# A hybrid decoder layer on one core: the first attention groups moved in the input projection, and the loads at the start of the last stage placed anew

## The chip, the core and the metric

The kernel runs on one core of a Trainium2 chip. The core has TensorE (PE in the profile; its weight loads are PEld), VectorE (DVE), ScalarE (ACT), GpSimd (POOL) and SyncE (SP), which work side by side and wait for each other through semaphores. DMA transfers are issued by SP, ACT or POOL; each of these works through its instructions in order, so a transfer that has to wait holds up all that its engine was given after it. The metric is the time of one execution on the device in microseconds (us); smaller is better.

## The reference

One layer of a decoder for 4096 new tokens of width 1024 and 64 sampled ones, in float32:

```python
h = _rmsnorm(x, g_pre)
z = h @ w_in                                   # 1024 x 2816
cb, cc, ch, cg, q, k, v, ag, mq, mg = _split_cols(z)
u = cc * ch                                    # A: gated short convolution, 256 channels
out_a = silu(cg) * cb * conv3(u)
o_b = window_attention(q, k, v, sink)          # B: 8 query heads, 2 key heads of 64, window 128
out_b = silu(ag) * o_b
o_c = memory_attention(mq, mk, mv)             # C: 4 heads of 64 into 256 memory tokens
out_c = silu(mg) * o_c
y = concat([out_a, out_b, out_c]) @ w_out      # 1024 x 1024
x = x + _rmsnorm(y, g_post)
```

Besides the new rows it returns the last keys, values and convolution rows, and the memory's keys and values.

## The kernel before

Every float32 product is made of three matmuls on a high and a low part of its operands: ACT casts the high part (`hi`, `mh`, `wo` first half), DVE subtracts for the low part (`lo`, `ml`, `wo` second half).

**The input projection** goes over 8 blocks of 520 tokens in three phases; each block and phase takes seven products of a fast matrix scheme (`PRODUCTS`). In the third phase a product has three quads of 12 matmuls (`product`, L381), so a step, one product of one block, has 36. Steps are numbered `n = 7 * (b - 1) + p` from -7 to 48 (`third_jobs`). Work of other kinds is hung into a step: a job of slot 0, 1 or 2 is written behind quad 0, 1 or 2. `evict` (L388) adds the accumulators into z on DVE; `finish_parts` casts z into two parts and stores them to `qd`, `finish_v` to `vd`, `finish_gate` and `finish_conv` to `md`. `v_load` and `v_turn` turn the value rows in steps `V_TURNS` and store them to `vn`.

**Attention** works on 16 chunks of 256 tokens, two groups of 128 queries each. A chunk's keys and queries are loaded by `chunk_load` (one issue for `kst`, two or four for `q`, all on POOL), its gates by `load_mix` (`mix`, or `place` for even chunks). Chunk 0 and the odd chunks share one buffer for keys and one for queries (`third["pre"]`). A group passes through these pieces:

- `bands` and `crosses`: scores on TensorE (`ws`, `xs`); `band_out` copies the window scores into the group's tile `s`, a copy on ACT (L1242) and a masked one on DVE (L1246);
- `band_max`, `band_exps`, `band_weights`, `cross_max`, `cross_exps`, `cross_weights`: softmax; the last is on POOL (L1295);
- `turn_band` (L1303) and `turn_cross` (L1307): DVE transposes 32 x 32 squares within `s`, and 16 transfers of 64 KB carry the squares into the tile `w` (L1312);
- `masks` (L1322): four selects on POOL that mask `w` and make `wd`;
- `values` (L1095, `pv`): products with the values (`vh` for loaded value rows, `halves`), then the gates are multiplied in.

`s` lives in one of two tiles: `pair` (single buffer of the pool `work`) for groups 0, 1, 2 and all even ones, the pool `sp` for the odd ones from 3. A new `s` waits until the 16 transfers of the last one have left. The transfers go through POOL for groups 0 and 1 and through SP from group 2 on.

Groups 0, 1 and 2 do all but the last pieces within the third phase: `EARLY` gives the step at which a group opens, `STAGES` and `PIECES` the steps after it.

**The last stage** takes 33 blocks of 128 rows (`Block.run`). A block is 48 matmuls of 128 x 512 (L1616, `y`), in two halves p of eight k with three products each. `events_of(i, block)` writes other work ahead of product k of half p. `values_and_scores(i)` makes the scores of group i + 3 and the values of group i + 1 (at the start of a block from block 2 on; after k = 2 in block 0, k = 3 in block 1). `turn(0, g)`, `turn(1, g)` and `turn(2, g)` are the two transposes and the masks. `split` makes `mh` and `ml` of a block's mixed rows; those of block 1 have their low part on POOL, all others on DVE. `query_loads` brings the later chunks from within `scores`. The output weights are loaded on POOL by `wo_load` in the last eight steps (raw tiles `wor`, the last three in the buffers `hx` of the input tiles) and split by `wo_split`, whose low part is on POOL for four of 16 tiles. `open_attention` lays the pools of the last stage over those of the projection; the first pool lies over `hx`.

The instructions of DVE, PE, SP, ACT and POOL stand in the order in which they are written (`written_order`), in the third phase and after it.

## Time and profile before

| | |
|---|---|
| median of three runs | 1494.8 us (1493.6 to 1497.38) |
| profiled execution | 1495.91 us, span 1494.2 us |
| granted clock of TensorE, mean | 0.997 |
| instructions | 30887 |
| third phase ends, last stage begins | at 945.6 us of the span |

The profile records one execution; its times count from the first instruction. A row of the timeline has start, length, engine, line, operation, output <- inputs, shape and how often; in brackets stands how long the engine had been idle and what ended that. SPq is SP's issuing of transfers. A row of stretches has the stretch, its length, the busy time of PE, PEld, DVE, ACT and POOL with the number of instructions, the granted clock, the DMA share and GB/s. A row by line has the least, median and greatest length in ns. Matmuls overlap and their ends are modelled, so PE shows as busy in places where it runs slowly.

### The profile page before, as it was taken

What the parts mean: (1) busy time and instruction counts of PE and PEld (TensorE: products, weight loads), DVE (VectorE), ACT (ScalarE), POOL (GpSimd) and SP (SyncE); (2) the same over time, 40 slices, a digit from 0 to 9 for tenths busy, and PEclk for the clock granted to TensorE, in tenths of its full rate; (3) what the DMA queues carried; (4) which work ended last, traced back from release to release, by engine and by line L of the source; (5) the groups of instructions that cost most, each with busy time, mean ns of one, the idle gap of its engine ahead of it and who ended that gap; (6) DMA issues with size and microseconds to landing.
All of it is one profiled execution on the core that took longest, in us unless ns stands there. A gap on an engine that the chain in (4) does not pass through costs nothing.

```text
span 1494.2 us, 30887 instructions
## 1 busy us (share of the span) xinstructions
PE 1465.3 (98%) x11459; PEld 1338.3 (90%) x11459; DVE 1209.0 (81%) x1888; ACT 758.4 (51%) x1869; POOL 447.4 (30%) x611
## 2 busy tenths in 40 slices
PE   9999999999999999999999999889999999999998
PEld 9999999999999999999999989767777777777766
DVE  6779888898987877797677768978988888888853
ACT  6776566466422222244545435645655655655542
POOL 0222332212300000000000332555556555565541
PEclk9999999999999999999999999999999999999999
DMA  9989999886864333257898987999999998899673
GB/s 256 195 241 226 292 288 275 229 286 241 236 204 145 135 122 129 100 216 229 281 287 273 291 259 242 326 234 224 215 250 221 235 234 222 211 222 243 203 205 109
DMA packets 213788, 337.27 MB, mean 226 GB/s; under 512 B 55301, under 2 KB 127365, under 8 KB 213605
## 3 DMA queue, kind: packets, MB, share of 16 engines
q1 hardware_dynamic: 159621, 226.42, 51.7%
q0 software_dynamic: 44944, 77.10, 21.0%
q10 hardware_dynamic: 9072, 31.77, 6.9%
q8 instruction: 91, 1.49, 0.5%
q14 instruction: 60, 0.49, 0.1%
HBM read 192.48 MB, written 110.15 MB: 203 GB/s over the span
## 4 chain that ended last, share of the span: by engine, by line
PE 63%; DMA 18%; DVE 7%; SPq 4%; issue 4%; POOL 2%; ACT 2%; ACTq 0%; POOLq 0%; DVEq 0%
PE c L381 46%; PE y L1616 11%; DMA w<-s 6%; SPq L1312 3%; PE pv L1095 3%; DMA mix<-md 2%; DMA xr<-in_x_p 1%; DMA place<-md 1%; PE ws L1095 1%; PE mem_acc L809 1%; DMA o_yp<-xr 1%; DMA vh<-vn 1%; DVE z L388 1%; DMA svm<-in_cmv 1%; DMA vd<-v 1%
## 5 line engine op out<-in xcount | busy, mean ns | idle before, releaser
L1616 PE MATMUL y<-wo,mh 128*128 128x512 f32 (+1 forms) x1040 | 329.3, 391 | 1.0 <-DVE s L1246 0.5
L388 DVE TENSOR_TENSOR z<-c,z 128x520 f32<-128x520 f32 (+1 forms) x308 | 193.6, 642 | 78.1 <-PE c L381 74.3
L1616 PEld LDWEIGHTS y<-wo,mh 128*128 128x128 f32 x1040 | 194.2, 188 | 54.3 <-DVE wmx L1255 5.0
L1616 PE MATMUL y<-wo,ml 128*128 128x512 f32 (+1 forms) x520 | 201.2, 387 | 0.5 <-POOL ml L1591 0.5
L1295 POOL TENSOR_SCALAR s<-s,xrd 128x256 f32<-128x256 f32 x128 | 61.2, 493 | 214.3 <-DVE xrd L1292 154.5
L1616 PEld LDWEIGHTS y<-wo,ml 128*128 128x128 f32 x520 | 97.8, 188 | 19.4 <-POOL ml L1591 0.9
L1265 ACT ACTIVATE s<-s,wnm 128x128 f32<-128x128 f32 x256 | 98.7, 387 | 0.0
L1242 ACT COPY s<-ws 128x256 f32<-128x256 f32 x128 | 41.1, 378 | 98.6 <-PE ws L1095 64.4
L1646 POOL TENSOR_TENSOR xr<-yn,xr 128x1024 f32<-128x1024 f32 x31 | 74.5, 2403 | 27.7 <-ACT yn L1645 22.7
L754 POOL MEMSET negs<- 128x1 f32 x1 | 0.1, 99 | 269.1 <-PE c L381 269.1
L1624 ACT ACTIVATE y<-y 128x512 f32<-128x512 f32 (+1 forms) x66 | 38.6, 585 | 58.4 <-DVE yn L1623 57.5
L1322 POOL TENSOR_SCALAR_AFFINE_SELECT wd<-w 128x512 f32<-128x512 f32 x64 | 52.9, 827 | 50.2 <-DMA w<-s 30.9
L1246 DVE COPY_PREDICATED s<-wmask,ws 128x256 f32<-128x256 uint8 x124 | 47.9, 439 | 21.4 <-ACT s L1242 20.0
L1623 DVE TENSOR_TENSOR yn<-y,gpost 128x512 f32<-128x512 f32 (+1 forms) x66 | 44.8, 679 | 21.8 <-PE y L1616 20.2
L1095 PEld LDWEIGHTS ws<-kst,q 64*128 64x128 f32 x768 | 48.2, 186 | 14.6 <-issue 9.9
L1095 PE MATMUL ws<-kst,q 64*128 64x256 f32 x768 | 56.0, 289 | 3.0 <-DVE s L1246 2.6
L1288 ACT ACTIVATE s<-xs,xnm 128x256 f32<-128x256 f32 x128 | 58.1, 461 | 1.0 <-DVE xnm L1282 1.0
L1322 POOL TENSOR_SCALAR_AFFINE_SELECT w<-w 128x512 f32<-128x512 f32 x64 | 56.1, 895 | 2.2
L390 ACT COPY z<-c 128x520 f32<-128x520 f32 (+1 forms) x44 | 24.4, 554 | 56.1 <-PE c L381 53.6
L1645 ACT ACTIVATE yn<-yn,yst 128x1024 f32<-128x1024 f32 x31 | 35.7, 1150 | 33.2 <-POOL yst L1637 33.2
L1265 ACT ACTIVATION_READ_ACCUMULATOR s<-s,wnm 128x1 f32 x256 | 47.9, 187 | 0.0
L185 POOL DMA_DIRECT2D md<-th x48 | 26.2, 548 | 64.8 <-DVE th L442 40.6
(957 smaller groups left out, 4986.9 us busy)
## 6 DMA issues: line engine op xcount, KB each, us to landing
w<-s SPq DMA_DIRECT2D x480, 64.0 KB
q<-qd POOLq DMA_DIRECT2D x30, 768.0 KB, 8.8
xr<-in_x_p SPq DMA_DIRECT2D x32, 512.0 KB
nat<-in_x_p SPq DMA_DIRECT2D x39, 416.0 KB
o_yp<-xr SPq DMA_DIRECT2D x31, 512.0 KB
md<-th POOLq DMA_DIRECT2D x48, 260.0 KB, 6.2
qd<-zh SPq DMA_DIRECT2D x48, 260.0 KB
qd<-z SPq DMA_DIRECT2D x48, 260.0 KB
```

The costliest lines, as they stand in the source:

```text
L381: TE.matmul(bank[:, :HW], l, r, start=first and i == 0, stop=last and i == 3 * KH - 1)
L388: add = lambda dst, other: V.tensor_tensor(dst, c, other, op=ALU.add)
L1095: ins = TE.matmul(o, w, x, **kw)
L1246: V.copy_predicated(to, squares(third["wmask"]), squares(s3[:, :, 0:P]))
L1265: S.activation(sm[:, h], sm[:, h], AF.Exp, bias=nm[:, h : h + 1], scale=SCALE, accum_out=den[:, h : h + 1])
L1288: S.activation(p[:, i], s[:, i].rearrange("p (a k j) -> p a k j", a=2, k=4), AF.Exp, bias=nm[:, i : i + 1], scale=SCALE, accum_out=den[:, ...
L1295: G.tensor_scalar(p[:, i], p[:, i], rd[:, i : i + 1], 0.5, op0=ALU.mult, op1=ALU.mult)
L1312: (DMA if b > 1 else G).dma_start(to[32 * k : 32 * k + 32, g], self.squares[32 * g : 32 * g + 32, k])
L1322: G.affine_select(out, src, pattern=[[32 * sign, 2], [0, 8], [sign, 32]], compare_op=op, fill=0.0, base=base * sign, channel_multiplier=-s ...
L1616: TE.matmul(acc, self.hl[l][:, k], wo[k][c0 // 512][:, r, c0 % 512 : c0 % 512 + c1 - c0], start=j == 0, stop=j == passes * KT - 1)
L1623: V.tensor_tensor(yn[:m, c0:c1], acc[:m], gpost[0][:m, c0:c1], op=ALU.mult)
L1646: total = G.tensor_tensor(self.xr, yn, self.xr, op=ALU.add)
```

## The change

- **First groups.** `EARLY` opens groups 0, 1 and 2 at steps 14, 23 and 33 in place of 17, 27 and 37. The transposes come in the stages 5 and 6 after it in place of 6 and 7, masks at 9 in place of 10, values at 14 and 15 in place of 16; the eight exponentials are split 6 and 2 in place of 4 and 4.
- **Their loads.** Chunk 0's keys and queries are loaded at step 10 (were in `first_chunk`, step 14), its values and gates at 12, `early_values` at step 20 (was 16), chunk 1 at 26 (was 29).
- **Buffers and queues.** Group 2's 16 transfers go through POOL in place of SP. From group 3 on the two tiles for `s` are exchanged: odd groups take `pair`, even ones `sp`; the sample's scores (`ssm`) move from `pair` to `sp`. In `open_attention` the pools `mixp` and `sp` change places, so that `mixp` is now the first.
- **End of the projection.** In the last step the weight tiles 14 and 15 are split in slot 2 in place of slot 1. The value rows 2 and 3 (`half_load`) are loaded before the last pending stores, and the pool `vp` is opened there.
- **Start of the last stage.** Chunk 2 is loaded before mix 1, and mix 1 through POOL in place of SP. Chunk 3 is loaded in block 0 (was block 1), mix 2 ahead of k = 6 of block 1's first half (was its second half). The low part of block 1 is computed on DVE.

```diff
-                            (14, 0, first_chunk), (16, 0, lambda: chunks[0].early_values()), (29, 0, lambda: chunk_load(1))):
+                            (10, 2, lambda: chunk_load(0)), (12, 0, first_chunk), (20, 2, lambda: chunks[0].early_values()), (26, 0, lambda: chunk_load(1))):
...
-    EARLY = {0: 17, 1: 27, 2: 37}
+    EARLY = {0: 14, 1: 23, 2: 33}
...
-              (3, 0, of("band_exps", range(0, 4))), (3, 0, of("early_cross_max")), (4, 0, of("band_exps", range(4, 8))),
-              (5, 0, of("early_cross_exps")), (5, 0, of("band_weights")), (6, 0, of("early_cross_weights")), (6, 0, of("turn_band")),
-              (7, 0, of("turn_cross")))
-    PIECES = {0: (*STAGES, (10, 0, of("masks")), (16, 0, of("values"))), 1: (*STAGES, (10, 0, of("masks")), (16, 0, of("values"))),
-              2: (*STAGES, (10, 0, of("masks")))}
+              (3, 0, of("band_exps", range(0, 6))), (3, 0, of("early_cross_max")), (4, 0, of("band_exps", range(6, 8))),
+              (4, 0, of("early_cross_exps")), (4, 1, of("band_weights")), (5, 0, of("early_cross_weights")), (5, 0, of("turn_band")),
+              (6, 0, of("turn_cross")), (9, 0, of("masks")))
+    PIECES = {0: (*STAGES, (14, 0, of("values"))), 1: (*STAGES, (15, 0, of("values"))), 2: STAGES}
...
-        chunk_load(0)
         chunk = chunks[0]
...
-                    slots[(0, 0, 1, 1)[n] if p == 6 else (0, 1, 1, 2)[n]].append(lambda j=j: wo_split(j))
+                    slots[(0, 0, 2, 2)[n] if p == 6 else (0, 1, 1, 2)[n]].append(lambda j=j: wo_split(j))
...
+        nonlocal vp
+        vp = ctx.enter_context(tc.tile_pool(name="vp", bufs=4, side="right"))
+        for n in range(2, 4):
+            half_load(n)
         for i in sorted(pending):
...
-        sp, bp, wd0 = left("sp"), left("bp"), left("wd0")
+        mixp, bp, wd0 = left("mixp"), left("bp"), left("wd0")
         left("gap").tile([P, NS], F32, name="gap")
-        bq, yq, wl, wd1, mixp, yp = left("bq"), left("yq"), left("wl"), left("wd1"), left("mixp"), left("yp", 2)
+        bq, yq, sp, wl, wd1, yp = left("bq"), left("yq"), left("sp"), left("wl"), left("wd1"), left("yp", 2)
...
-            (G if self.c == 2 else DMA).dma_start(self.mix, md[:, :, self.ts].rearrange("k p n -> p k n"))
+            (G if 0 < self.c < 3 else DMA).dma_start(self.mix, md[:, :, self.ts].rearrange("k p n -> p k n"))
...
-            t = sp.tile([P, 2 * D], F32, tag="s", name=f"s{b}") if b % 2 and b > 1 else pair(f"s{b}")
+            t = pair(f"s{b}") if b % 2 or b < 3 else sp.tile([P, 2 * D], F32, tag="s", name=f"s{b}")
...
-                    (DMA if b > 1 else G).dma_start(to[32 * k : 32 * k + 32, g], self.squares[32 * g : 32 * g + 32, k])
+                    (DMA if b > 2 else G).dma_start(to[32 * k : 32 * k + 32, g], self.squares[32 * g : 32 * g + 32, k])
...
-        ssm = pair("ssm")
+        ssm = sp.tile([P, 2 * D], F32, tag="s", name="ssm")
...
-                (G if b == 1 else V).tensor_tensor(lo, src, f(hi), op=ALU.subtract)
+                V.tensor_tensor(lo, src, f(hi), op=ALU.subtract)
...
+    chunk_load(2)
     chunks[1].load_mix()
-    chunk_load(2)
-    for n in range(2, 4):
-        half_load(n)
...
+        if i == 0:
+            at(1, 1, chunk_load, 3)
         if i == 1:
-            at(1, 1, chunk_load, 3)
-            at(1, 1, lambda: chunks[2].load_mix())
+            at(0, 6, lambda: chunks[2].load_mix())
```

More of the change, by code (lines that the diff above doesn't have):

```diff
@@ L1055, in open_attention @@
     def open_attention():
-        nonlocal ps, mixp, wp, wl, vp, bp, bq, yp, yq, sp
+        nonlocal ps, mixp, wp, wl, bp, bq, yp, yq, sp
         own.close()
@@ L1062, in open_attention @@
         ps = {tag: ctx.enter_context(tc.tile_pool(name=f"ps{tag}", bufs=1, space=bass.MemoryType.PSUM)) for tag in (*range(4), "pv", 4, 5)}
-        vp = ctx.enter_context(tc.tile_pool(name="vp", bufs=4, side="right"))
         left = lambda name, bufs=1: att.enter_context(tc.tile_pool(name=name, bufs=bufs))
-        sp, bp, wd0 = left("sp"), left("bp"), left("wd0")
+        mixp, bp, wd0 = left("mixp"), left("bp"), left("wd0")
         left("gap").tile([P, NS], F32, name="gap")
-        bq, yq, wl, wd1, mixp, yp = left("bq"), left("yq"), left("wl"), left("wd1"), left("mixp"), left("yp", 2)
+        bq, yq, sp, wl, wd1, yp = left("bq"), left("yq"), left("sp"), left("wl"), left("wd1"), left("yp", 2)
         wp = wd0, wd1
```

## The prediction, made before the changed kernel ran

> **What bounds the kernel now.** I read the page's busy row first, then TensorE's own rows in order of time, kept to those with idle time before them (and four without, used below), then the stretches around the places found.
>
> ```profile
> PE 1465.3 (98%) x11459; PEld 1338.3 (90%) x11459; DVE 1209.0 (81%) x1888; ACT 758.4 (51%) x1869; POOL 447.4 (30%) x611
> ```
> TensorE is the bound, and the change touches no matmul. It can move the time only through TensorE's idle time and the slow clock after it. Nearly all of what it can reach sits in two places.
>
> ```profile
> 892.80 1.50 PE L1095 MATMUL ws<-kst,q 64*128 64x256 f32 x12 [2.56 <-DVE s L1246]
> ...
> 945.60 0.39 PE L1616 MATMUL y<-wo,mh 128*128 128x512 f32 x1
> ...
> 951.06 0.98 PE L1095 MATMUL xs<-mk,q 64*128 64x256 f32 x11 [1.45 <-DVE z L388]
> 956.21 0.50 PE L1616 MATMUL y<-wo,mh 128*128 128x512 f32 x1 [0.52 <-DVE s L1246]
> 962.65 0.50 PE L1616 MATMUL y<-wo,ml 128*128 128x512 f32 x1 [0.48 <-POOL ml L1591]
> 965.39 0.38 PE L1095 MATMUL ws<-kst,q 64*128 64x256 f32 x2
> 966.12 1.58 PE L1095 MATMUL ws<-kst,q 64*128 64x256 f32 x22 [0.35 <-DMA q<-qd]
> 968.10 0.97 PE L1095 MATMUL xs<-mk,q 64*128 64x256 f32 x11 [0.28 <-DVE s L1246]
> 971.73 0.65 PE L1095 MATMUL pv<-w,vh 128*64 128x256 f32 x4 [1.21 <-DMA vh<-vn]
> 981.30 0.98 PE L1095 MATMUL ws<-kst,q 64*128 64x256 f32 x12
> 984.43 1.09 PE L1095 MATMUL pv<-w,mv 128*64 128x128 f32 x16 [0.72 <-ACT y L1624]
> 1005.80 1.44 PE L1095 MATMUL pv<-w,mv 128*64 128x128 f32 x16 [4.63 <-ACT y L1624]
> ...
> 1021.06 1.69 PE L1095 MATMUL ws<-kst,q 64*128 64x256 f32 x24
> ```
> ```profile
> 887.00:900.00 13.00, 10.44 (x77) 9.86 (x76) 7.24 (x14) 4.37 (x8) 2.85 (x4) 0.87 0.78 249
> 1000.00:1011.00 11.00, 6.37 (x57) 4.05 (x56) 5.55 (x12) 4.72 (x17) 5.11 (x6) 0.84 1.48 314
> 972.50:982.50 10.00, 10.00 (x64) 7.91 (x62) 8.70 (x16) 6.10 (x25) 5.16 (x5) 1.00 0.40 99
> 987.00:1012.00 25.00, 20.31 (x133) 15.12 (x126) 14.75 (x33) 13.48 (x52) 15.41 (x18) 0.93 1.37 299
> ```
>
> The bracket is the idle time and what ended it; in the stretches the third number from the end is the granted clock, the last two are DMA share and GB/s. Steps of the third phase are counted back from 945.6, 36 matmuls each. The first wait is in step 38: 2.56 us idle and 13.00 x (1 - 0.87) = 1.7 us of slow clock, 4.25 us. The other eight, blocks 0 to 3 of the last stage, are 9.64 us, with 11.00 x (1 - 0.84) = 1.8 us of slow clock after the longest. Together 15.7 us, 1.0% of the time.
>
> **The change part by part.** *First groups.* The wait in step 38: group 2's scores go into the one buffer that group 1 used, and group 1's 16 transfers had not left it.
>
> ```profile
> 872.73 1.24 DVE L1307 STREAM_TRANSPOSE s<-s 128x1024 f32<-128x1024 f32 x1
> ```
> ```profile
> 874.57 7.15 POOL L1312 DMA_DIRECT2D w<-s  x14 [3.96 <-DVE z L424]
> ```
> ```profile
> 891.90 0.37 ACT L1242 COPY s<-ws 128x256 f32<-128x256 f32 x1 [7.39 <-DMA w<-s]
> ```
>
> From the transpose's end (873.97) to the copy (891.90) are 17.9 us. That made TensorE 2.56 us late, so 15.4 us would have been in time, over three steps. The change puts group 1's turn at step 29 and group 2 at step 33: four steps, some 4.3 us more. The wait is gone: -4.25 us. But group 0 turns at step 20 and group 1 opens at 23: three steps again. What did group 0 take before (turn at 24)?
>
> ```profile
> 824.05 1.24 DVE L1307 STREAM_TRANSPOSE s<-s 128x1024 f32<-128x1024 f32 x1
> ```
> ```profile
> 839.21 1.54 POOL L1322 TENSOR_SCALAR_AFFINE_SELECT wd<-w 128x512 f32<-128x512 f32 x2 [2.31 <-DMA w<-s]
> ```
>
> 825.29 to 839.2: 13.9 us, in time. Step 20, though, is the last product of its block, as step 34 was and step 24 was not; the stores that follow it and the value-row loads one and three steps later (the turns at 23 and 25, at 37 and 39) fall beside the transfers in both. So I take step 34's 17.9 us as the nearer row: 17.9 - 15.4 - 0.4 (the two value transposes that now lie inside) = 2.1 us of wait at step 24. Whether the slow clock follows lies between the 1.45 us wait, after which none shows, and the 2.56 us wait, after which it does; I take half of 1.7. Term +3.0 us, between 0 (by 13.9) and +5.3 (by the 19.4 us of group 4 below, with the clock). The six steps in place of eight and the split of the exponentials move the same instructions; TensorE had no wait on them and DVE has room (a stretch of steps 20 to 23 is 14.04 us busy of 17.4). I put this at nothing.
>
> ```profile
> 803.50:820.90 17.40, 17.40 (x147) 17.40 (x146) 14.04 (x25) 12.88 (x36) 0.98 (x3) 1.00 0.79 260
> ```
>
> *Chunk 0, its values and chunk 1 sooner.* These loads had landed without a wait of TensorE, and come sooner now; nothing.
>
> *Group 2's turn at 39, its masks at 42, its transfers from SP to POOL.* Before, they fell into steps 44 to 48 and POOL stood behind them:
>
> ```profile
> 947.18 1.84 POOL L1322 TENSOR_SCALAR_AFFINE_SELECT wd<-w 128x512 f32<-128x512 f32 x2 [6.11 <-DMA w<-s]
> 949.09 2.17 POOL L1322 TENSOR_SCALAR_AFFINE_SELECT w<-w 128x512 f32<-128x512 f32 x2
> 951.23 3.41 POOL L204 TENSOR_TENSOR wo<-wor,wo 128x512 fp32r<-128x512 f32 x2
> 954.94 0.74 POOL L1128 DMA_DIRECT2D kst<-qd  x1 [0.30 <-POOL wo L204]
> ```
> ```profile
> 954.67 1.20 ACT L1242 COPY s<-ws 128x256 f32<-128x256 f32 x4 [3.00 <-POOL wo L204]
> ```
> ```profile
> 947.47 2.08 DVE L204 TENSOR_TENSOR wo<-wor,wo 128x512 fp32r<-128x512 f32 x2
> ...
> 950.59 0.42 DVE L388 TENSOR_TENSOR z<-c,z 128x260 f32<-128x260 f32 x1
> ```
>
> POOL waited 6.11 us for the transfers, so its share of the output weights and chunk 2's loads came late, and group 3's scores, laid over those weights' raw tiles, waited 3.00 us on ACT. With masks at 42 and group 3 in the other buffer this chain is gone: the 0.52 us and 0.35 us waits with it. The two weight splits of 2.08 us now stand behind the last eviction (950.59), which then ends about 2 us sooner, more than the 1.45 us it was late. The low part of block 1 goes to DVE, where the others take 1.2 us:
>
> ```profile
> L1591 DVE TENSOR_TENSOR ml<-place,mh x15: 1181/1184/1648, 944.5 to 1426.3; 128x1024 fp32r<-128x1024 f32 x15
> L1591 POOL TENSOR_TENSOR ml<-place,mh x1: 2404/2404/2404, 960.2 to 960.2; 128x1024 fp32r<-128x1024 f32 x1
> ```
>
> DVE, full until 957, is relieved by more than it is given: 0.48 us gone. Value rows 2 and 3 are asked for before the last stores, two issues on SP of some 0.6 us that the stores wait for and nobody behind them: 1.21 us gone. Term: 1.45 + 0.52 + 0.48 + 0.35 + 1.21 = -4.0 us; were DVE still late, -2.0. On POOL group 2's 16 issues (0.51 each) stand ahead of its masks alone, which wait for them anyway. Chunk 2's five, mix 1 (from SP) and chunk 3's three, 0.74 to 0.85 us each, are some 7 us ahead of group 3's weights and the next block's output; POOL has given up 2.40 us of low part and does the 4.01 us of masks and most of the 3.41 us of weights earlier, so I count nothing, and 1 us within the bounds above if that cover is thin.
>
> *Chunk 3 and mix 2.* They stood behind group 3's masks on POOL and then ran with chunk 4 just when group 4's transfers had to leave group 6's buffer:
>
> ```profile
> 970.37 11.28 SPq L1312 DMA_DIRECT2D w<-s  x16
> ...
> 985.15 13.12 SPq L1312 DMA_DIRECT2D w<-s  x16
> ```
> ```profile
> 983.13 0.65 ACT L1242 COPY s<-ws 128x256 f32<-128x256 f32 x2 [4.11 <-DMA w<-s]
> ...
> 1004.51 0.65 ACT L1242 COPY s<-ws 128x256 f32<-128x256 f32 x2 [5.76 <-DMA w<-s]
> ```
>
> 19.4 us for group 4, at 299 GB/s all around; 12.8 us for group 3, with DMA at a share of 0.40. Moving chunk 3 (by its shape 1.6 MB of queries and 0.4 of keys) and mix 2 (1.0 MB) from 987 to about 963 and later lets group 4 end in time: 4.63 + 1.8 = -6.4 us. **What is late next is group 3**, whose buffer group 5 needs a block later. Its first transfer went 5.0 us after its block's score matmuls began (965.39), 0.6 of it TensorE's own waits. The score matmuls begin 2.7 us into a block (12 matmuls of 0.227), so the transfers go at 7.1 to 7.3 us. A block without waits lasts 16.0 us (the four from 1021 on), and the copy may come 1.1 us into the next (981.30 + 1.83, less the 0.72 it was late). 16.0 + 1.1 - 7.2 = 9.9 us, where 12.8 are needed even in quiet. Before, TensorE's waits in block 1 made the room; they are what is taken away.
>
> ```profile
> 1021.00:1037.00 16.00, 16.00 (x117) 12.71 (x116) 13.79 (x25) 9.66 (x35) 7.92 (x10) 1.00 1.32 270
> ```
>
> So this wait grows from 0.72 us to 2.9 us in quiet and 9.5 us at group 4's 19.4. The 3 MB now beside it and its own 1 MB are 13.5 us at 299 GB/s, about its own length, so I add 1.1 us to the quiet row: 4.0 us, and 1.7 us of slow clock. Term 4.0 + 1.7 - 0.7 = +5.0 us, between +2.2 (no slow clock) and +10.5. It also gives group 4 that much more time, which keeps its own wait away even at 17 us.
>
> The four blocks lasted 1021.06 - 945.60 = 75.5 us against 13.5 + 3 x 16.0 = 61.5: 14.0 us, of which the waits and the clock explain 11.4. Of the other 2.6, matmuls slow without a recorded wait, I take half: -1.2 us (0 to -2.6).
>
> Sum: -4.25 + 3.0 - 4.0 - 6.4 + 5.0 - 1.2 = -7.8 us. The profiled execution took 1495.91 us (span 1494.2), 1.1 above the median of the three, so 1488.1 there and **1487.0** as a median.
>
> [...] The page TensorE: Matmul & The Clock Gate (Part 1) gives an idle window of about 3.4 us before the clock halves. By it neither 2.1 nor 2.56 us need cost clock and the sum would be 0.85 us lower; the trace shows the slow clock after 2.56 us.
>
> **The rivals.** *No new wait at step 24* (chance 0.24). Group 0's transfers keep the 13.9 us, and group 3's stay near 12.8. The 3.0 us of step 24 and 1 us of the other go: 1483. For it: DMA moved 260 GB/s in steps 20 to 23, below the 299 above.
>
> *The wait only moves from block 3 to block 2* (0.20). Chunk 3, mix 2 and group 3's transfers collide as group 4's did; at 17 us the wait is 7.1 instead of 4.0, at 19.4 it is 9.5. That is 3.1 to 5.5 us more: 1490 to 1492.5. Against it: SP alone needs 11 us, so DMA has slack.
>
> *Output weights late, slower than before* (0.13). POOL loads them from step 43 on, now behind masks that wait for group 2's transfers. Before, the first went here:
>
> ```profile
> 924.24 3.26 POOL L941 DMA_DIRECT2D wor<-in_w_out  x6
> ```
>
> That is 0.3 us into step 44, five steps of 4.35 us after step 39. The turn ends 3.7 us into its step (873.97 in step 34, which began at 870.3), and the masks take 4.1, so for the same start group 2's transfers must land 21.8 + 0.3 - 3.7 - 4.1 = 14.3 us after the turn. At 17.9 the loads come 3.6 us late, ACT's casts with them, and the high and low parts of the last two steps stand behind those casts. The last step's low part had little room:
>
> ```profile
> 939.75 1.23 DVE L372 TENSOR_TENSOR lo_7T<-x_7T,hi_7T 128x1040 fp32r<-128x1040 f32 x1
> ```
>
> It ended at 940.98, and the last step's second matmul, which reads it, came 4.2 us before 945.6, at 941.4. Each us late beyond 0.5 is a us of TensorE, with 1.7 us of slow clock for each of two waits (3.4): 7.8 us are eaten when the transfers land 14.3 + 0.5 + 4.4 = 19.2 us after the turn, and at 22 to 27 us it is 1498 to 1503. Against it: the 1 MB that ran beside the weights is gone, and 19.4 is the longest seen.
>
> *The edits do not do what they say* (0.03): a queue that runs ahead of its program's place issues a load when its buffer and data are free, wherever it is written; if that held for all of them nothing would move: 1495. Against it: the masks' 6.11 us are a wait that the new places take away.
>
> **How the numbers follow.** Forecast 0.40: 1484.5 to 1490. What can be told from no change is 0.3%, 4.5 us, so faster means under 1490.3: 0.40 + 0.24 + 0.07 of the second rival at its low end, 0.71. Same: the rest of the second, 0.13, with 0.03 of the third and the last 0.03, 0.19. Slower, over 1499.3: 0.10. The range for 8 in 10 leaves out half of the first rival's lower side and most of the third: 1480.5 to 1495.0.
>
> **What would show it.** In the changed profile: no wait of ws in step 34; a wait of ws at step 24 of 0 to 4 us; no wait on z, ml, q or vh in blocks 0 and 1; pv's wait in block 2 grown to 3 to 5 us and the one in block 3 gone. The prediction is wrong if block 3's 4.63 us stay, if TensorE waits for hi, lo or wo in steps 45 to 48, or if the four blocks take less than 64 or more than 73 us.

## The result and the profile after

The changed kernel takes 1496.85 us (median of 14 runs, 1491.39 to 1497.92) beside 1495.7 us for the kernel before (14 runs, 1492.17 to 1499.6). The ratio is 1.0002 with a 95% interval of 0.9992 to 1.0013: no change that can be measured, where 7.8 us less had been forecast. Its profiled execution took 1495.76 us, span 1494.0.

Two profiles whose totals agree can still differ in every part, so the span is cut at places that both have: the start of step 13 (the changed kernel opens its first group in step 14), the last product's end, and the score matmuls of blocks 2, 3 and 4. The lengths are worked out from the starts of TensorE's matmuls:

| us | before | changed | difference | forecast |
|---|---|---|---|---|
| up to step 13 | 769.25 | 767.21 | -2.04 | 0 |
| steps 13 to 48 | 176.52 | 178.89 | +2.37 | -1.25 |
| of it step 38 beyond its own matmuls | 4.46 | 0 | -4.46 | -4.25 |
| of it step 24 beyond its own matmuls | 0 | 6.75 | +6.75 | +3.0 |
| blocks 0 and 1 (last product's end to block 2's scores) | 35.53 | 33.68 | -1.85 | -4.0 |
| block 2 | 17.14 | 23.76 | +6.62 | +5.0 |
| block 3 | 22.62 | 17.04 | -5.58 | -6.4 |
| block 4 to the end | 473.14 | 473.47 | +0.33 | 0 |

(Step 38 lasted 9.87 us before; step 24 lasts 12.16 now. With half a group's scores in it, as both have, a step without a wait lasts 5.41. The -1.2 us that the forecast booked on unrecorded slowness belongs to the blocks too.) The first row is scatter: in seven of the kernels below, which are the same program as the changed one up to there, step 13 starts anywhere from 768.77 to 772.65 us. A difference of some us in the total of one profiled execution therefore says nothing; the parts say more (how far they can be trusted stands under the table of the experiments).

TensorE's rows with idle time in the changed kernel (start, duration, then the idle time before and what ended it):

```profile
825.11 1.98 PE L1096 MATMUL ws<-kst,q 64*128 64x256 f32 x12 [3.77 <-DVE s L1247]
...
949.58 1.69 PE L1096 MATMUL ws<-kst,q 64*128 64x256 f32 x24 [0.81 <-DVE z L388]
964.75 1.57 PE L1096 MATMUL ws<-kst,q 64*128 64x256 f32 x22 [0.64 <-DMA q<-qd]
974.15 0.47 PE L1617 MATMUL y<-wo,mh 128*128 128x512 f32 x1 [1.22 <-DVE mix L1368]
988.23 1.98 PE L1096 MATMUL pv<-w,mv 128*64 128x128 f32 x16 [6.04 <-ACT y L1625]
...
1006.56 1.09 PE L1096 MATMUL pv<-w,mv 128*64 128x128 f32 x16 [0.61 <-ACT y L1625]
```

The 2.56 us of step 38 and the 4.63 us of block 3 are gone (0.61 us is left there). In their places stand 3.77 us at step 24 and 6.04 us in block 2: two waits went, two larger ones came. Stretches around them show the clock (third number from the end); the first pair is the changed kernel, the second the kernel before:

```profile
824.50:831.30 6.80, 6.19 (x31) 5.92 (x32) 5.74 (x10) 3.02 (x7) 3.40 (x5) 0.50 0.79 198
985.00:991.70 6.70, 3.47 (x24) 2.48 (x24) 3.31 (x8) 2.93 (x8) 4.58 (x7) 0.50 0.45 152
```
```profile
893.70:897.10 3.40, 3.40 (x20) 3.18 (x17) 3.40 (x6) 1.51 (x4) 1.19 (x2) 0.51 0.84 285
1006.40:1009.80 3.40, 3.40 (x26) 1.59 (x22) 1.98 (x5) 1.73 (x5) 2.14 (x4) 0.50 1.78 307
```

Before, each of the two waits was followed by 3.4 us at half clock. Now each comes with 6.7 to 6.8 us of it, which begins while the wait is still on. TensorE was at work for 6.19 and 3.47 us of them; half of that, 3.1 and 1.7 us, is lost.

**Step 24, read backwards.** ACT's copy is what frees the scores, and it waits for group 0's transfers:

```profile
824.21 0.37 ACT L1243 COPY s<-ws 128x256 f32<-128x256 f32 x1 [8.60 <-DMA w<-s]
```
```profile
801.16 1.23 DVE L1304 STREAM_TRANSPOSE s<-s 128x1024 f32<-128x1024 f32 x1
802.31 1.00 DVE L388 TENSOR_TENSOR z<-c,z 128x520 f32<-128x520 f32 x2
803.23 1.22 DVE L372 TENSOR_TENSOR lo_4B<-x_4B,hi_4B 128x1040 fp32r<-128x1040 f32 x1
804.37 1.24 DVE L1308 STREAM_TRANSPOSE s<-s 128x1024 f32<-128x1024 f32 x1
```

The second turn ends at 805.61 and the copy starts 18.6 us later. Step 20 starts at 801.17, so the turn ends 4.4 us into it, where the forecast took 3.7 us from step 34, group 1's turn: DVE has no gap between these four rows. Group 0's turn was as late before, when it stood in step 24: it ended at 825.29, 4.5 us after that step's start at 820.80.

**Block 2.** SP's issues of group 3's transfers and ACT's copy for group 5, which needs that buffer:

```profile
968.76 11.84 SPq L1313 DMA_DIRECT2D w<-s  x16
```
```profile
986.93 0.65 ACT L1243 COPY s<-ws 128x256 f32<-128x256 f32 x2 [9.41 <-DMA vh<-vn]
```

18.2 us, where it was 12.8 before and 13.9 forecast. (The row names a value row's load; group 3's transfers, which share SP's queue with it, are what the copy needs: POOL's masks, which read only them, start at 986.98.)

### The profile page after: what moved, and what is told of

It is laid out like the page before. It is cut to its first block, busy times and chain, and to the rows that moved or that the text cites. A ratio compares the mean times of both kernels' runs of the same rounds, so it can differ in the third digit from the quotient of the medians.

```text
span 1494.0 us, 30880 instructions
## 1 busy us (share of the span) xinstructions
PE 1465.0 (98%) x11459; PEld 1339.6 (90%) x11459; DVE 1205.4 (81%) x1889; ACT 758.6 (51%) x1869; POOL 454.3 (30%) x627
## 3 DMA queue, kind: packets, MB, share of 16 engines
q0 software_dynamic: 45728, 79.20, 21.4%
## 4 chain that ended last, share of the span: by engine, by line
PE 63%; DMA 18%; DVE 7%; issue 5%; SPq 4%; POOL 2%; ACT 2%; ACTq 0%; DVEq 0%; POOLq 0%
PE c L381 47%; PE y L1617 10%; DMA w<-s 6%; PE pv L1096 3%; DMA place<-md 3%; SPq L1313 3%; DMA vh<-vn 2%; DMA mix<-md 1%; PE ws L1096 1%; DMA xr<-in_x_p 1%; DMA wor<-in_w_out 1%; DVE z L388 1%; PE mem_acc L809 1%; DMA q<-qd 1%; DMA vd<-v 1%
## 5 line engine op out<-in xcount | busy, mean ns | idle before, releaser
L388 DVE TENSOR_TENSOR z<-c,z 128x520 f32<-128x520 f32 (+1 forms) x308 | 193.8, 644 | 79.1 <-PE c L381 75.4
L1647 POOL TENSOR_TENSOR xr<-yn,xr 128x1024 f32<-128x1024 f32 x31 | 74.5, 2403 | 26.3 <-ACT yn L1646 22.7
L1096 PEld LDWEIGHTS ws<-kst,q 64*128 64x128 f32 x768 | 48.7, 188 | 16.6 <-issue 9.9
L294 ACT ACTIVATE nat<-nat 104x1024 f32<-104x1024 f32 x40 | 42.2, 1055 | 9.5 <-DMA nat<-in_x_p 9.5
```

The costliest lines, as they stand in the source:

```text
L388: add = lambda dst, other: V.tensor_tensor(dst, c, other, op=ALU.add)
L1096: ins = TE.matmul(o, w, x, **kw)
L1647: total = G.tensor_tensor(self.xr, yn, self.xr, op=ALU.add)
```

## Experiments

The ratios are to runs of the kernel before on the same chip in the same series; medians of different series are not to be compared. "blocks" is from the last product's end to block 4's score matmuls. Waits are those of TensorE over 0.25 us, each block counted from its score matmuls on. Steps, blocks and waits come from one profiled execution each.

| kernel | steps 13-48 | blocks | waits in block 1 / 2 / 3 | median us | ratio (95%) |
|---|---|---|---|---|---|
| before | 176.5 | 75.3 | 1.8 / 0.7 / 4.6 | 1495.7 | 1 |
| changed | 178.9 | 74.5 | 1.9 / 6.0 / 0.6 | 1496.85 | 1.0002 (0.9992-1.0013) |
| e1_open_later | 180.6 | 71.7 | 1.3 / 5.6 / 0 | 1499.09 | 1.0024 (1.0012-1.0037) |
| e2_loads_back | 179.8 | 72.8 | 2.2 / 0 / 4.4 | 1496.86 | 1.0017 (1.0000-1.0034) |
| e3_turn_first | 179.4 | 76.3 | 4.2 / 2.4 / 2.9 | 1500.79 | 1.0025 (1.0003-1.0047) |
| e4_both | 180.9 | 71.9 | 2.7 / 3.2 / 1.4 | 1497.73 | 1.0009 (0.9995-1.0022) |
| e5_later_clean | 175.5 | 74.8 | 2.2 / 5.5 / 1.8 | 1494.68 | 0.9981 (0.9963-1.0000) |
| e7_due | 175.3 | 72.0 | 2.4 / 3.7 / 0 | 1491.96 | 0.9975 (0.9958-0.9993) |
| e6_due_and_turn | 175.4 | 72.3 | 2.3 / 2.0 / 1.8 | 1493.0 | 0.9977 (0.9959-0.9995) |
| e10_first_only | 173.2 | 74.9 | 1.4 / 5.6 / 0 | 1491.77 | 0.9974 (0.9960-0.9988) |
| e8_first_sooner | 172.8 | 71.1 | 2.4 / 2.3 / 0.7 | 1492.03 | 0.9964 (0.9946-0.9983) |
| e9_first_sooner_turn | 173.7 | 73.5 | 3.1 / 2.9 / 0.3 | 1490.15 | 0.9964 (0.9949-0.9980) |
| e12_mix_sooner | 172.6 | 75.4 | 0.8 / 5.4 / 2.4 | 1492.6 | 0.9972 (0.9955-0.9988) |
| e11_two_queues | 173.5 | 84.1 | 2.5 / 14.8 / 0 | 1503.77 | 1.0039 (1.0025-1.0053) |

How well do such parts repeat? Steps 13 to 48 are one program in the changed kernel, e2 and e3 (178.9, 179.8 and 179.4 us), and in the five kernels that open group 0 at step 13 (172.6 to 173.7): they repeat within about 1 us. The last stage is one program in the changed kernel, e1, e5 and e10, which differ only ahead of it, and its blocks took 74.5, 71.7, 74.8 and 74.9 us; in e3 and e4 76.3 and 71.9. So a difference of 3 to 4 us in the blocks shows nothing by itself; the rows have to show its cause.

### Step 24: is it only a matter of time?

```diff
-    EARLY = {0: 14, 1: 23, 2: 33}
+    EARLY = {0: 14, 1: 24, 2: 34}
```

> Groups 1 and 2 open at steps 24 and 34, one step later than in the changed kernel. Theory: the changed kernel's wait at step 24 (3.77 us, then 6.8 us of slow clock that cost some 3 us) is only the time by which group 0's transfers are late for group 1; a step later (4.3 us) they are in time, so both go, nothing else grows by over 1 us, and the time falls by 6 to 7 us, to about 1490 where the changed kernel has 1496.5. Rival: the wait comes back a step later, because the transfers slow down too (over 2 us of wait at step 25, gain under 3 us). Second rival: group 2's masks, now at step 43, hold up POOL's loads of the output weights, and TensorE waits in steps 44 to 48: the gain is eaten and the time is 1495 or more.

The wait at step 24 is gone and does not come back at step 25. But the kernel is slower: 2.05 us appear at step 28 and 6.4 us in steps 46 and 47 (7.26 and 7.84 us long, where 4.35 is usual). TensorE's rows, then POOL's:

```profile
848.49 1.09 PE L1096 MATMUL pv<-w,mv 128*64 128x128 f32 x16 [2.05 <-ACT s L1289]
...
940.72 0.59 PE L381 MATMUL c<-hi_7B,w_0S 128*128 128x260 f32 x1 [2.76 <-ACT hi_7B L371]
942.23 0.59 PE L381 MATMUL c<-lo_7B,w_0S 128*128 128x260 f32 x1 [0.92 <-DVE lo_7B L372]
```
```profile
912.32 4.45 POOL L1313 DMA_DIRECT2D w<-s  x9 [4.50 <-PE c L381]
...
927.35 1.51 POOL L1323 TENSOR_SCALAR_AFFINE_SELECT wd<-w 128x512 f32<-128x512 f32 x2 [6.23 <-DMA w<-s]
928.93 1.40 POOL L1323 TENSOR_SCALAR_AFFINE_SELECT w<-w 128x512 f32<-128x512 f32 x2
930.29 1.11 POOL L939 DMA_DIRECT2D wor<-in_w_out  x2
```

This is the third rival of the prediction, one step later: POOL waits 6.23 us for group 2's transfers, and the loads of the output weights stand behind the masks. The masks start 15.6 us after the turn's end (911.76), and the turn stands 4.9 us nearer to the start of step 44 than in the changed kernel. On the scale of that rival this is 20.5 us, past the 19.2 for which it worked out 7.8 us eaten. The second rival of this run, the one with the masks, was right. The wait at step 28 is a shared PSUM buffer: group 0's values need the buffer that group 1's cross scores hold until ACT has read them.

On top of e1:

```diff
-    PIECES = {0: (*STAGES, (14, 0, of("values"))), 1: (*STAGES, (15, 0, of("values"))), 2: STAGES}
+    PIECES = {0: (*STAGES, (15, 0, of("values"))), 1: (*STAGES, (15, 0, of("values"))), 2: (*STAGES[:-1], (11, 0, of("masks")))}
```

> Groups 1 and 2 open one step later as in e1_open_later, but group 0's values stand at step 29 instead of 28 and group 2's masks at step 45 instead of 43, behind most of POOL's output weight loads. Theory: the losses of e1 (2.1 us at step 28, 6.4 us in steps 46 and 47) were only the score buffer in PSUM that the values shared and the masks ahead of the loads; both go, the gain at step 24 stays, and steps 14 to 48 take 167 to 169 us (before 171.8, changed 174.1, e1 175.9). The time is 1489 to 1492. Rival: DMA has no room in steps 40 to 48, the weights are late wherever the masks stand, and steps 45 to 48 still lose over 3 us. Second rival: the gain comes back as waits in blocks 0 to 3 (together over 12 us against 9.7 in the changed kernel), and the time is 1495 or more.

Step 28's wait is gone and step 46 is whole; steps 14 to 48 take 170.8 us (the table's 175.5 less step 13), 5.1 less than e1, but steps 47 and 48 still lose 2.9 us and step 24 0.8 us (for a low part on DVE). So the theory held for the direction and not for its 167 to 169 us, nor for its time (1494.68 us, ratio 0.9981, where 1489 to 1492 was expected). The last six issues of output weight loads now stand behind the masks and leave POOL at 937.82. What helps the steps more is to move group 0 and to leave groups 1 and 2 where the change puts them:

```diff
-    EARLY = {0: 14, 1: 23, 2: 33}
+    EARLY = {0: 13, 1: 23, 2: 33}
...
-                            (10, 2, lambda: chunk_load(0)), ...
+                            (9, 2, lambda: chunk_load(0)), ...
...
-    PIECES = {0: (*STAGES, (14, 0, of("values"))), 1: (*STAGES, (15, 0, of("values"))), 2: STAGES}
+    PIECES = {0: (*STAGES, (15, 0, of("values"))), 1: (*STAGES, (15, 0, of("values"))), 2: STAGES}
```

> Group 0 opens one step sooner (13) than in the changed kernel, groups 1 and 2 stay at 23 and 33, the last stage stays as changed. Theory: the transfers of group 0 then have one step (4.3 us) more, so the 3.77 us wait at step 24 and the 3.0 us of slow clock after it go, as in e1, but without touching group 2's masks and the output weights; steps 14 to 48 take 167 to 168.5 us (changed 174.1, e5 170.8), and the time falls by 5 to 7 us below the changed kernel, to about 1490. Rival: a step sooner the softmax of group 0 falls on the steps in which DVE is full (4.9 to 5.5 us busy in steps 5, 7 and 13) and TensorE waits there instead (over 2 us in steps 12 to 20). Second rival: the turn is late on DVE in any case, the transfers start less than 2 us sooner, and the wait at step 24 stays at 2 us or more.

Steps 14 to 48 take 167.3 us, but 1.1 us of score matmuls have moved from step 14 to 13; by the table's steps 13 to 48 it is 5.7 us less than the changed kernel, within the theory's 5 to 7. The time is 0.9974 of the kernel before, where the changed kernel has 1.0002: some 4 us less, with intervals that do not meet. The turn on DVE, the first transfers on POOL, and the score matmuls of step 24, which have no idle time before them:

```profile
803.03 1.23 DVE L1308 STREAM_TRANSPOSE s<-s 128x1024 f32<-128x1024 f32 x1
```
```profile
804.56 6.50 POOL L1313 DMA_DIRECT2D w<-s  x13 [4.14 <-DVE s L1308]
```
```profile
823.68 0.97 PE L1096 MATMUL ws<-kst,q 64*128 64x256 f32 x12
```

Step 20 starts at 803.54 here, so the turn ends 0.7 us into it instead of 4.4. The 6.75 us of step 24 are gone, and the four blocks do not take them back (74.9 us beside 74.5). Steps 47 and 48 take 0.9 us more than in the changed kernel, as they do in e2 and e3 (0.6 and 1.1), which have its steps.

### Block 2 and block 3: what makes the transfers late?

```diff
-        if i == 0:
-            at(1, 1, chunk_load, 3)
         if i == 1:
-            at(0, 6, lambda: chunks[2].load_mix())
+            at(1, 1, chunk_load, 3)
+            at(1, 1, lambda: chunks[2].load_mix())
```

> Chunk 3's and mix 2's loads go back to the second half of block 1, the rest of the change stays. Theory: what makes group 3's transfers late for block 2 is these 3 MB beside them. Then the wait in block 2 falls from 6.04 us to under 2 us, the wait in block 3 comes back with 4 to 6 us and one stretch of slow clock, and the time is the same within 2 us. Rival: the transfers are late because SP has only so many of them on the way at a time, whatever runs beside them; then the wait in block 2 stays above 4.5 us, block 3's comes on top, and the time rises by 4 us or more.

The rows of this kernel: SP's issues for groups 3 and 4, the copy that waits for group 3's, and TensorE in block 3.

```profile
971.32 10.81 SPq L1313 DMA_DIRECT2D w<-s  x16
985.85 12.99 SPq L1313 DMA_DIRECT2D w<-s  x16
```
```profile
983.64 0.65 ACT L1243 COPY s<-ws 128x256 f32<-128x256 f32 x2 [3.36 <-PE ws L1096]
```
```profile
999.98 1.58 PE L1096 MATMUL ws<-kst,q 64*128 64x256 f32 x22 [0.58 <-DMA q<-qd]
...
1006.08 1.09 PE L1096 MATMUL pv<-w,mv 128*64 128x128 f32 x16 [3.80 <-ACT y L1625]
```

Group 3's transfers take at most 12.3 us instead of 18.2: the copy no longer waits for them, and block 2 has no wait; block 3 has 3.8 us. The DMA rows of the two stretches, this kernel first, then the changed one:

```profile
971.00:984.00 13.00, 11.60 (x78) 8.62 (x76) 9.15 (x20) 7.46 (x31) 5.46 (x6) 1.00 0.60 183
```
```profile
969.00:986.00 17.00, 11.98 (x84) 9.02 (x80) 10.22 (x20) 6.77 (x28) 6.10 (x6) 0.97 1.29 314
```

The same 16 transfers need 12.3 us at a DMA share of 0.60 and 18.2 at 1.29 (the share adds up the times of all packets, so it can pass 1). The theory is shown: the 3 MB of chunk 3 and mix 2 make group 3 late where the change puts them, and group 4 where they were. The packets of the traces say the same for more kernels. From the first issue to the end of group 3's last packet it takes 11.9 to 12.4 us with 0.5 to 0.9 MB of other data moved meanwhile (before, e2), 15.6 to 16.6 with 3.0 to 3.4 MB (e7, e8, e12), 16.4 to 17.3 with 4.0 to 4.5 MB (e10, e5, e1, changed), and 18.9 to 20.4 with 4.3 to 5.5 MB where the transfers start sooner (e3, e4, e6, e9).

```diff
         if i == 1:
             at(0, 0, turn, 0, 3)
+            at(0, 0, turn, 1, 3)
...
-            if self.b == 4:
-                turn(1, 3)
```

> Group 3's second turn stands before group 4's band copies on DVE, in a gap in which DVE is idle for 1.8 us, so its transfers can start at about 965.7 instead of 968.8 in span time. Theory: the wait in block 2 is the plain length of that chain, so it falls by about 3 us, from 6.04 to about 3, with one stretch of slow clock in place of two, and the time falls by 3 to 5 us. Rival: the loads beside them (mix 2 landed at 986.4, after the last transfer) set when the last one lands; then the transfers only take longer, the wait stays above 5 us, and the time changes by under 1 us.

Block 2's wait falls to 2.36 us as the theory had it, yet the time does not fall: the transfers take 21.0 us (971.32 to the copy at 992.30) instead of 18.2, as the rival had it, and others wait.

```profile
971.75 2.18 PE L1096 MATMUL ws<-kst,q 64*128 64x256 f32 x22 [1.39 <-DMA q<-qd]
983.19 0.47 PE L1615 MATMUL y<-wo,mh 128*128 128x512 f32 x1 [2.23 <-DVE mix L1366]
...
993.60 1.09 PE L1096 MATMUL pv<-w,mv 128*64 128x128 f32 x16 [2.36 <-ACT y L1623]
...
1012.99 1.63 PE L1096 MATMUL pv<-w,mv 128*64 128x128 f32 x16 [2.91 <-DMA w<-s]
```

> The later opening of groups 1 and 2 and the earlier second turn of group 3 together. Theory: they lie 150 us apart and add up: 9 to 12 us less than the changed kernel, about 1486, a ratio of 0.994 to the kernel before. Rival: whatever of the two gains fails alone fails here too, so the time is that of the better one alone.

Its rival came true: e1's step 24 gain and its loss in steps 46 and 47 are both there, and 0.9995 to 1.0022 is no change. Next, on top of e5, the loads were put by due time, which was to be between the two groups' transfers:

```diff
-        if i == 0:
-            at(1, 1, chunk_load, 3)
         if i == 1:
-            at(0, 6, lambda: chunks[2].load_mix())
+            at(0, 6, chunk_load, 3)
+            at(1, 0, lambda: chunks[2].load_mix())
```

> As e5_later_clean, with chunk 3's loads behind block 0's output on POOL in block 1 (about 8 us later than in the changed kernel) and mix 2 behind group 4's cross weights (8 us later too), so that they run between group 3's and group 4's transfers. Theory: waits follow from which loads run beside the transfers; here each runs in the gap, so block 2's wait is under 3.5 us and block 3's under 2 us, 3 to 5 us less than e5. Rival: DMA is full over these blocks as a whole, so that the waits of blocks 1 to 3 together stay at 6.5 us or more, as in every kernel so far, and only their places change.

> As e7_due, with group 3's second turn ahead of group 4's band copies (3 us sooner), as in e3_turn_first. Theory: the waits of blocks 1 to 3 together fall below 4 us, and the time is 3 us or more below e7. Rival: group 3's transfers then run beside mix 1, which block 1's gates wait for (2.2 us in e3), and the sum of the waits stays at 6.5 us or more.

The waits of blocks 1 to 3 fall to 6.0 and 6.1 us, from 9.5 in e5: below the rivals' 6.5, far from e6's theory of under 4. In e7 block 2's 3.7 us miss the 3.5 expected, block 3's wait is gone. Beside e5, e7's blocks take 2.8 us less, and its median is 2.7 us lower, with intervals that overlap; the blocks of one program differ by as much, so a gain of the new places is not shown. They don't do what was meant either: in e7 POOL issues chunk 3's loads at 974.8 to 976.5, in the midst of group 3's transfers (969.95 to 986.91). The early turn on top brings nothing. With group 0 opened sooner:

> As e10_first_only, with chunk 3's and mix 2's loads where e7_due has them. Theory: e7's gain in blocks 0 to 3 (2.5 us less than the changed kernel) and e10's gain add up: 2 to 3 us below e10 and 3 us below e7, about 1488. Rival: blocks 0 to 3 give the gain back, since they start 7 us sooner with the same bytes to move; then it is the same as e10 within 1 us.

> As e8_first_sooner, with group 3's second turn sooner as in e6. Theory by e6 beside e7 (blocks 0 to 3 took 88.2 against 87.9 us): no difference to e8 beyond 1 us, because what group 3's transfers gain, mix 1 and group 4's transfers lose. Rival: it takes another 2 us or more off block 2's wait without a loss elsewhere.

These have the lowest ratio, 0.9964 of the kernel before (0.9946 to 0.9983 and 0.9949 to 0.9980), 5 to 6 us. Against e10 that is no gain that can be told: the intervals overlap, and in one series the medians are 1491.77 (e10), 1492.03 (e8) and 1490.15 us (e9), as e8's rival had it. e9 is the same as e8, as expected. In the profile e8's blocks are 3.8 us below e10's, and that execution, at 1487.68 us, was far below e8's median. Group 3's transfers take 17.2 us in e8 and 17.3 in e10.

SP's issues in e10 and in e8, then in e8 the block output that waits, and the gate on DVE that it waits for:

```profile
967.18 12.18 SPq L1313 DMA_DIRECT2D w<-s  x16
```
```profile
962.72 10.65 SPq L1313 DMA_DIRECT2D w<-s  x16
```
```profile
969.24 0.47 PE L1617 MATMUL y<-wo,mh 128*128 128x512 f32 x1 [2.35 <-DVE mix L1368]
981.23 1.09 PE L1096 MATMUL pv<-w,mv 128*64 128x128 f32 x16 [2.34 <-ACT y L1625]
```
```profile
968.07 0.42 DVE L1337 TENSOR_TENSOR mix<-mix,pv 128x256 f32<-128x256 f32 x1 [3.88 <-DMA mix<-md]
```

Counted from the last product's end (942.67 and 941.28) the transfers begin at 24.5 us in e10 and 21.4 in e8. In e10 block 1's score matmuls wait 1.42 us for chunk 2's queries, the clock is halved for 3.4 us after it, and the turn behind them is late; in e8 that wait is gone. So in these two executions the difference is an earlier start, not a shorter transfer. That the new places of chunk 3 and mix 2 bring it is not shown: e11, the same program as e8 up to there, waits 0.50 us for these queries, and e9 1.64. What e8 still has is mix 1, for which DVE waits 3.88 us:

```diff
-    chunk_load(2)
-    chunks[1].load_mix()
+    first_loads = query_loads(2)
+    for fn in (*first_loads[:2], chunks[1].load_mix, first_loads[2]):
+        fn()
```

> As e8_first_sooner, with mix 1's load ahead of the second half of chunk 2's queries on POOL (that half is first used a block later). Theory: block 1's gates wait for mix 1 (DVE 3.88 us, TensorE 2.35 us in e8) because it stands behind all of chunk 2's loads; with some 0.8 MB of queries behind it instead of ahead it lands about 2 us sooner, TensorE's wait in block 1 falls below 1 us, and the time falls by 1 to 2 us. Rival: the two loads share the DMA engines whichever is issued first, mix 1 lands within 0.7 us of where it did, and nothing changes; or the second half of the queries is now late for group 5 in block 2.

The gate no longer waits, and neither does block 1's output; block 2 pays for it:

```profile
969.17 0.42 DVE L1337 TENSOR_TENSOR mix<-mix,pv 128x256 f32<-128x256 f32 x1
```
```profile
983.81 1.98 PE L1096 MATMUL pv<-w,mv 128*64 128x128 f32 x16 [5.44 <-ACT y L1625]
```

The theory was right about mix 1; the 1 to 2 us less do not show in the time (1492.6 beside 1492.03 us, intervals that overlap). TensorE's 2.35 us in block 1 had been room for group 3's transfers. Counted from the last product's end, the copy for group 5 goes at 38.7 us in e8 and 38.9 in e12, but block 2 begins at 35.2 and 32.3: its wait goes from 2.34 to 5.44 us, block 3's from 0.68 to 2.39, and the blocks take 75.4 us. Last, the number of queues, on top of e8:

```diff
-                    (DMA if b > 2 else G).dma_start(to[32 * k : 32 * k + 32, g], self.squares[32 * g : 32 * g + 32, k])
+                    ((DMA, S)[k % 2] if 2 < b < 5 else DMA if b > 2 else G).dma_start(to[32 * k : 32 * k + 32, g], self.squares[32 * g : 32 * g + 32, k])
```

> As e8_first_sooner, with every second of the 32 transfers of groups 3 and 4 issued from ACT's queue instead of SP's, so that twice as many can be on the way at a time. Theory: what is on the DMA engines beside them sets when the last transfer lands (12.4 to 12.8 us from the first issue to the next use in quiet, 17.2 in e8, 20.8 in e9); then a second queue brings the issues earlier and the last landing by less than 2 us, and the time stays within 2 us of e8. Rival: how many SP may have on the way sets it; then group 3's 17.2 us fall to 13 or less, block 2's wait of 2.3 us goes, and the time falls by 2 to 4 us, unless ACT, which issues for some 2.7 us ahead of block 0's scaling, comes late itself.

SP's half of group 3's issues, a stretch just after them, POOL up to the masks (ACTq is ACT's issuing), then ACT around group 4's, then TensorE:

```profile
967.18 8.21 SPq L1313 DMA_DIRECT2D w<-s  x8
```
```profile
976.60:978.60 2.00, 2.00 (x9) 1.64 (x8) 0.00 (x0) 2.00 (x13) 2.00 (x1) 0.86 0.00 0
```
```profile
978.66 0.81 POOL L1129 DMA_DIRECT2D kst<-qd  x1
979.47 1.67 POOL L1136 DMA_DIRECT2D q<-qd  x2
981.75 2.81 POOL L1296 TENSOR_SCALAR s<-s,xrd 128x256 f32<-128x256 f32 x4 [0.61 <-DVE xrd L1293]
984.50 0.94 POOL L1144 DMA_DIRECT2D place<-md  x1
985.46 1.54 POOL L1323 TENSOR_SCALAR_AFFINE_SELECT wd<-w 128x512 f32<-128x512 f32 x2
```
```profile
986.71 10.09 ACTq L1313 DMA_DIRECT2D w<-s  x8
997.00 0.65 ACT L1243 COPY s<-ws 128x256 f32<-128x256 f32 x2 [14.22 <-DMA w<-s]
```
```profile
998.29 1.97 PE L1096 MATMUL pv<-w,mv 128*64 128x128 f32 x16 [13.66 <-ACT y L1625]
```

The issues of both queues end 8.2 us after the first, instead of 10.7, and at 976.6 the DMA engines stand still: group 3's transfers have landed within 9.4 us of their first issue. POOL's masks start 18.3 us after it, but they wait for nothing; POOL has other work ahead of them. So the rival has a share of the truth: with next to nothing beside them, two queues need 9.4 us where SP alone needs 11.9 to 12.4 (e2, before). What two queues would do beside chunk 3's loads this run cannot say, since POOL issues those here at 978.66, after the landing. The early landing doesn't help, and the time doesn't stay: group 4's issues on ACT have to wait for the turn and then take 10.09 us, and everything on ACT stands behind them, the copies that TensorE needs too. TensorE waits 13.66 us for this alone.

## Why the prediction was wrong

**Step 38** (-4.25 us) was right: the wait and its slow clock are gone.

**Step 24** has the largest miss: the right place with the wrong size, +6.75 us, where the forecast took 3.0 and bounded it by 5.3. Three terms of it were too small. The room: its 15.4 us come from group 1's turn, which ends 3.7 us into its step, and with 0.4 us more they make 15.8; group 0's turn ends 4.4 us into it, and the room was 14.8 us (824.21 - 3.77 - 805.61). Group 0's own turn, which the forecast shows at 824.05, was already that late, so "the six steps in place of eight" are not what it had wrong. The need: the transfers took 18.6 us instead of 17.9; why stays open. So the wait was 3.77 instead of 2.1 us. And the bound of the slow clock, 1.7 us, came from two rows with one stretch of 3.4 us each; the wait of 3.77 us brought two and cost 3.1. e1 and e10, which give a step more in two ways, show that nothing but time was lacking there.

**Blocks 0 and 1** gave 1.85 us of the 4.0, just outside the bound of 2.0. The waits on the weights (0.52), the value rows (1.21) and mostly on POOL's low part (0.48, now 0.33 for one on DVE) went, z's shrank from 1.45 to 0.81, the queries' grew from 0.35 to 0.64, and a new one came: 1.22 us for block 1's gates. The step that failed is the one on POOL's queue, "so I count nothing": mix 1, moved from SP to stand behind chunk 2's five loads, is late. The changed kernel's row names another engine; in e2 and e8, with mix 1 in the same place, DVE's wait names its load (2.95 and 3.88 us), and e12, which only moves that load, is without it. (e10 has no wait there either, after 1.42 us of waiting for the queries.)

**Block 3** (-5.6 against -6.4) was right, and so was most of the -1.2 us: 74.5 - 61.5 us leave 1.6 us beyond waits (9.65) and clock (1.7), where 2.6 had been.

**Block 2** failed in the step "I add 1.1 us to the quiet row: 4.0 us". The transfers took 18.2 us, not 13.9. That the wait was 6.04 us and not over 8 is luck: the room was 12.1 us instead of 9.9, since TensorE's waits in block 1, which the forecast took away, stayed (1.86 us). The argument against the second rival, that SP's issues need 11 us and DMA has slack, read the share of 0.40 in the quiet stretch as capacity left over; it was low because nothing else was asked for. With chunk 3 and mix 2 beside them the share is 1.29, and the 12 us become 18.2 (e2 and the changed kernel), and 21.0 where they start sooner, while mix 1 is still on its way (e3). So for the last stage the second rival came true, "the wait only moves from block 3 to block 2": the waits of blocks 1 to 3 were 7.2 us together before and 8.5 after.

Without the scatter ahead of step 13 the parts give +2.4 - 0.8 = +1.6 us against -7.8. Of the 9.4 us, 3.6 lie in the steps and 5.8 in the blocks, which repeat only within 3 to 4 us. The **third rival** stayed away: group 2's masks started 13.7 us after the turn's end (905.97 to 919.70), under the 14.3 us that it needs; e1 shows its mechanism at 20.5 us, with 6.4 us eaten. That the edits do nothing was wrong in each part and right in the sum, by chance.

What stays open: why the waits of blocks 1 to 3 don't fall below some 5.4 us in any order tried, while block 2's can be 0; whether fewer bytes in these blocks would do it was not tried. So does the cause of TensorE's wait for a low part in step -2 (0.34 us before, 0.5 to 1.4 in the kernels with chunk 0's loads moved).

## What to carry to other kernels

A buffer that is handed on by transfers has no fixed length: take it from a stretch with the traffic that will be there after the change (12.3 us in quiet, 18.2 beside 3 MB here), and when a load is moved, ask whose transfers it now runs beside. A wait that is removed was room for the next chain (e8 and e12): price a stretch as a whole, and name the next thing that becomes late until one has slack. Take a room from the row of the same group, not from a neighbour's (3.7 us for 4.4 at step 24). Where a chain is short of time, start what feeds it sooner (group 0 one step: 5.7 us less in the steps) rather than its user later, which here only handed the lateness on (e1).

## What the runs showed of the hardware

The slow clock comes in pieces, and on a fixed grid. Its changes stand at 893.77, 897.18, 1006.41 and 1009.82 us in the kernel before and at 824.51, 831.34, 984.94 and 991.77 in the changed one: within each kernel they are whole multiples of 3.413 us apart. What counts is TensorE's idle time in one window of this grid. Two windows of the kernel before, from its 2.56 us wait, after which the clock is halved, and from its 1.45 us wait, after which it is not:

```profile
890.36:893.77 3.41, 0.97 (x11) 0.82 (x12) 1.46 (x4) 1.87 (x4) 1.73 (x3) 1.00 0.32 100
948.38:951.79 3.41, 1.96 (x32) 1.76 (x28) 3.41 (x6) 1.87 (x4) 3.34 (x4) 1.00 0.98 369
```

In the 14 traces (from 40 to 1470 us) each of the 25 windows at full clock that were idle for over 54% ended in half clock, none that was idle for under 47%, and in between 4 of 11. The wait of 3.77 us had 3.2 us in one window; the next, already at half clock, was idle for another 17%, and full clock came back only at the end of the one after it, which was wholly busy: 6.8 us of half clock. The cost thus doesn't grow with the wait in a straight line: 1.7 us after 2.56, 3.1 after 3.77, and 1.7 after 6.04, since half of that slow time was idle anyway. The Trainium skill, page TensorE: Matmul & The Clock Gate, section "What's actually happening", describes windows of 3413 ns that run freely and halve the clock after an idle one; the grid agrees with it, but a window need not be wholly idle: 2.45 of its 3.41 us were enough here.

An engine that issues transfers for another's sake is held by them. SP took 10.7 to 15.5 us for the 16 issues of group 3 or 4 and has no arithmetic of its own that could stand behind them; ACT took 10.09 us for eight, and TensorE lost 13.66 us.
